# Row softmax on one core: row maximum added, tiles of sixteen rows per partition in three buffers

## The chip, the cores and the metric

The kernel runs on one core of one Trainium2 chip. The metric is the device time of one execution in microseconds (us); lower is better. VectorE is called DVE here, ScalarE is called ACT, and SP is the engine that issues the loads.

A run more than 1.5% above the fastest of the same kernel counts as slow.

## The reference

```python
x = randn(32, 512, 1024) as float32      # 16384 rows of 1024
temperature = 0.5

def reference(x, temperature):
    scaled = x / temperature
    shifted = scaled - max(scaled, axis=-1)
    e = exp(shifted)
    return e / sum(e, axis=-1)           # float32
```

67.1 MB are read and 67.1 MB are written.

## The kernel before

It leaves out the maximum. A tile has four rows per partition (2.1 MB, written 2 MB below, as the profile does), and eight tiles may be in flight. ACT does the exponential and the row sum, DVE the reciprocal and the multiplication.

```python
K_MAIN = 4; SPLIT_LAST = 4
data = tile_pool(name="data", bufs=8)
for it, (g0, K) in enumerate(sched):                 # 32 tiles
    xtile = data.tile([P, K, d], float32)
    nc.sync.dma_start(out=xtile, in_=xv)             # load, issued by SP
    for j in range(K):
        nc.scalar.activation(xtile[:, j, :], xtile[:, j, :], Exp,
                             scale=scale, accum_out=sums[:, j:j+1])
    nc.vector.reciprocal(recip, sums)
    for j in range(K):
        nc.vector.tensor_scalar_mul(xtile[:, j, :], in0=xtile[:, j, :],
                                    scalar1=recip[:, j:j+1])
    # ... cut: the last four tiles are stored in two halves
    nc.scalar.dma_start(out=ov, in_=xtile)           # store, issued by ACT
```

The program is plain text in this order, but the order in which an engine runs it need not be the order of the text: in the profile below ACT starts exponentials of tile 1 at 13.41 us and issues the store of tile 0 at 15.81 us.

The softmax here doesn't subtract the row's maximum and nothing guards it: scores larger than these inputs give would overflow.

Of the kernel before, what the change touches and what calls it, by code (L numbers as in the profile page):

```python
# [1 line left out]

# [4 lines left out]


@with_exitstack  # L10
def kernel(
    ctx: ExitStack,
    tc: tile.TileContext,
    x: bass.AP,
    temperature: bass.AP,
    out: bass.AP,
):
    nc = tc.nc
    scale = 1.0 / float(temperature)

    P = 128
    xf = x.flatten_outer_dims()
    of = out.flatten_outer_dims()
    n, d = xf.shape
    nrowgroups = n // P

    K_MAIN = 4
    SPLIT_LAST = 4
    sched = []
    g = 0  # L30
    while g < nrowgroups:
        k = min(K_MAIN, nrowgroups - g)
        sched.append((g, k))
        g += k
    ntiles = len(sched)

    data = ctx.enter_context(tc.tile_pool(name="data", bufs=8))
    stats = ctx.enter_context(tc.tile_pool(name="stats", bufs=16))

    for it, (g0, K) in enumerate(sched):  # L40
        rows = P * K
        r0 = g0 * P
        xv = xf[r0 : r0 + rows, :].rearrange("(p k) d -> p (k d)", p=P, k=K)
        ov = of[r0 : r0 + rows, :].rearrange("(p k) d -> p k d", p=P, k=K)

        xtile = data.tile([P, K, d], mybir.dt.float32)
        nc.sync.dma_start(out=xtile.rearrange("p k d -> p (k d)"), in_=xv)  # L47

        sums = stats.tile([P, K], mybir.dt.float32)
        recip = stats.tile([P, K], mybir.dt.float32)  # L50
        for j in range(K):
            nc.scalar.activation(  # L52
                xtile[:, j, :],
                xtile[:, j, :],
                mybir.ActivationFunctionType.Exp,
                scale=scale,
                accum_out=sums[:, j : j + 1],
            )
        nc.vector.reciprocal(recip, sums)  # L59
        for j in range(K):  # L60
            nc.vector.tensor_scalar_mul(  # L61
                xtile[:, j, :], in0=xtile[:, j, :], scalar1=recip[:, j : j + 1]
            )

        if it >= ntiles - SPLIT_LAST and K > 1:
            h = K // 2
            nc.scalar.dma_start(out=ov[:, :h, :], in_=xtile[:, :h, :])  # L67
            nc.sync.dma_start(out=ov[:, h:, :], in_=xtile[:, h:, :])
        else:
            nc.scalar.dma_start(out=ov, in_=xtile)  # L70


# [1 line left out]
_INS = ['x', 'temperature']  # L74
_OUTS = [((32, 512, 1024), 'float32')]
#: Inputs that are plain numbers.
_NUMBERS = {'temperature': 0.5}


# [26 lines left out]
```

## Time and profile before

| | before |
|---|---|
| time, median | 319.57 us (319.5 to 319.85) |
| span in the profile | 317.8 us |
| DVE busy / ACT busy | 93.4 us / 138.0 us |
| DMA engines busy, both queues | 52.9% + 46.3% = 99.2% of the span |

These lines are from the page of the kernel before: the busy time of each engine, the busy tenths of the DMA engines in 40 slices of the span, the rate in the same slices, the two DMA queues (q1 loads and some stores, q10 stores), and who owns the chain that ended last.

```profile
span 317.8 us, 636 instructions
DVE 93.4 (29%) x160; ACT 138.0 (43%) x257; POOL 0.2 (0%) x4
DMA  7999999999999999999999999999999999999996
GB/s 297 429 394 429 431 431 434 435 433 433 433 429 429 432 429 429 429 429 431 429 433 434 433 435 431 429 433 431 431 429 429 431 429 431 437 429 430 422 426 271
q1 hardware_dynamic: 5184, 71.31, 52.9%
q10 hardware_dynamic: 4608, 62.92, 46.3%
DMA 91%; ACT 1%; SPq 1%; DVE 1%; issue 0%; DVEq 0%; ACTq 0%
```

The DMA engines are busy from the first slice to the last. DVE and ACT are busy 29% and 43%.

The timeline of the kernel before, ACT and its DMA issues alone (start us, duration, engine, line, operation), shows the order of the text being left:

```profile
13.41 1.06 ACT L52 ACTIVATE xtile<-xtile 128x1024 f32<-128x1024 f32 x1 [0.62 <-DMA xtile<-in_x_dram]
...
15.50 1.04 ACT L52 ACTIVATE xtile<-xtile 128x1024 f32<-128x1024 f32 x1
15.81 0.37 ACTq L70 DMA_DIRECT2D out_dram<-xtile  x1
```

The exponential at 13.41 us belongs to tile 1. The DMA issue at 15.81 us is the store of tile 0, which the text lists before it.

### The profile page before, as it was taken

What the parts mean: (1) busy time and instruction counts of PE and PEld (TensorE: products, weight loads), DVE (VectorE), ACT (ScalarE), POOL (GpSimd) and SP (SyncE); (2) the same over time, 40 slices, a digit from 0 to 9 for tenths busy, and PEclk for the clock granted to TensorE, in tenths of its full rate; (3) what the DMA queues carried; (4) which work ended last, traced back from release to release, by engine and by line L of the source; (5) the groups of instructions that cost most, each with busy time, mean ns of one, the idle gap of its engine ahead of it and who ended that gap; (6) DMA issues with size and microseconds to landing.
All of it is one profiled execution on the core that took longest, in us unless ns stands there. A gap on an engine that the chain in (4) does not pass through costs nothing.

```text
span 317.8 us, 636 instructions
## 1 busy us (share of the span) xinstructions
DVE 93.4 (29%) x160; ACT 138.0 (43%) x257; POOL 0.2 (0%) x4
## 2 busy tenths in 40 slices
DVE  0352333312300517631333213333123003733300
ACT  1875334554321739655334553345543106852500
POOL 0000000000000000000000000000000000000000
DMA  7999999999999999999999999999999999999996
GB/s 297 429 394 429 431 431 434 435 433 433 433 429 429 432 429 429 429 429 431 429 433 434 433 435 431 429 433 431 431 429 429 431 429 431 437 429 430 422 426 271
DMA packets 9797, 134.26 MB, mean 422 GB/s; under 512 B 1088, under 2 KB 1088, under 8 KB 1088
## 3 DMA queue, kind: packets, MB, share of 16 engines
q1 hardware_dynamic: 5184, 71.31, 52.9%
q10 hardware_dynamic: 4608, 62.92, 46.3%
q14 instruction: 5, 0.04, 0.0%
HBM read 67.11 MB, written 67.11 MB: 422 GB/s over the span
## 4 chain that ended last, share of the span: by engine, by line
DMA 91%; ACT 1%; SPq 1%; DVE 1%; issue 0%; DVEq 0%; ACTq 0%
DMA xtile<-in_x_dram 55%; DMA out_dram<-xtile 36%; ACT xtile L52 1%; SPq L47 1%; DVE xtile L61 1%; DVEq L101 0%; ACTq L67 0%; DVE recip L59 0%; ACTq L52 0%; ACTq L70 0%
## 5 line engine op out<-in xcount | busy, mean ns | idle before, releaser
L52 ACT ACTIVATE xtile<-xtile 128x1024 f32<-128x1024 f32 x128 | 133.5, 1044 | 159.3 <-DMA xtile<-in_x_dram 158.2
L61 DVE TENSOR_SCALAR xtile<-xtile,recip 128x1024 f32<-128x1024 f32 x128 | 87.7, 749 | 1.1
L59 DVE RECIPROCAL recip<-sums 128x4 f32<-128x4 f32 x32 | 5.7, 178 | 206.5 <-ACT xtile L52 206.5
L52 ACT ACTIVATION_READ_ACCUMULATOR xtile<-xtile 128x1 f32 x128 | 23.8, 186 | 0.0
L52 ACT ACT_TABLE_LOAD x1 | 1.3, 1283 | 0.7 <-PEq L87 0.7
L87 POOL MEMSET const-bfloat16-1.0<- 128x1 bf16 x1 | 0.1, 101 | 0.0
L87 POOL MEMSET const-uint8-127<- 128x1 uint8 x1 | 0.1, 101 | 0.0
L87 POOL MEMSET const-float32-0.0<- 128x1 f32 x1 | 0.1, 98 | 0.2 <-issue 0.2
L87 POOL MEMSET const-float32-1.0<- 128x1 f32 x1 | 0.1, 98 | 0.0
## 6 DMA issues: line engine op xcount, KB each, us to landing
xtile<-in_x_dram SPq DMA_DIRECT2D x32, 2048.0 KB, 31.3
out_dram<-xtile ACTq DMA_DIRECT2D x28, 2048.0 KB, 24.2
out_dram<-xtile ACTq DMA_DIRECT2D x4, 1024.0 KB, 22.7
out_dram<-xtile SPq DMA_DIRECT2D x4, 1024.0 KB, 14.9
```

Of the source, the lines that this page charges most:

```text
L47: nc.sync.dma_start(out=xtile.rearrange("p k d -> p (k d)"), in_=xv)
L52: nc.scalar.activation(xtile[:, j, :], xtile[:, j, :], mybir.ActivationFunctionType.Exp, scale=scale, accum_out=sums[:, j : j + 1],)
L59: nc.vector.reciprocal(recip, sums)
L61: nc.vector.tensor_scalar_mul(xtile[:, j, :], in0=xtile[:, j, :], scalar1=recip[:, j : j + 1])
L87: nc = _bacc.Bacc("TRN2", target_bir_lowering=False, num_devices=1)
```

## The change

The intent is a numerically safe softmax (the maximum is subtracted), paid for with larger transfers: sixteen rows per partition, 8.4 MB per load and store, 64 KiB per partition in one piece, three buffers. Cut to its core:

```diff
+def _softmax_rows(nc, stats, xt, j0, n, scale):        # n = 4 rows
+    nc.vector.tensor_reduce(out=top, in_=xt[:, j0:j0+n, :], axis=X, op=max)
+    nc.vector.tensor_scalar_mul(bias, in0=top, scalar1=-scale)
+    for j in range(n):
+        nc.scalar.activation(..., Exp, bias=bias[:, j:j+1], scale=scale,
+                             accum_out=sums[:, j:j+1])
+    nc.vector.reciprocal(recip, sums)
+    for j in range(n):
+        nc.vector.tensor_scalar_mul(...)               # as before
 ...
-    K_MAIN = 4
+    plan = [[16]] * 7 + [[8, 8]]                       # rows per store, by tile
-    data = tile_pool(name="data", bufs=8)
+    data = tile_pool(name="data", bufs=3)
 ...
+        nc.sync.dma_start(out=xt, in_=xv)
+        for k in stores:
+            for a in range(j, j + k, 4):
+                _softmax_rows(nc, stats, xt, a, 4, scale)
+            nc.scalar.dma_start(out=ov[:, j:j+k, :], in_=xt[:, j:j+k, :])
```

A tile now has four groups of four rows. "The maxima of a tile" below are its four reductions on DVE, "the multiplies" its sixteen multiplications.

More of the change, by code (lines that the diff above doesn't have):

```diff
@@ L7 @@
 from concourse._compat import with_exitstack
+def _softmax_rows(nc, stats, xt, j0, n, scale):
+    f32 = mybir.dt.float32
+    P = xt.shape[0]
+    top = stats.tile([P, n], f32, name="top")
+    bias = stats.tile([P, n], f32, name="bias")
+    sums = stats.tile([P, n], f32, name="sums")
+    recip = stats.tile([P, n], f32, name="recip")
+    nc.vector.tensor_reduce(
+        out=top,
+        in_=xt[:, j0 : j0 + n, :],
+        axis=mybir.AxisListType.X,
+        op=mybir.AluOpType.max if scale > 0 else mybir.AluOpType.min,
+    )
+    nc.vector.tensor_scalar_mul(bias, in0=top, scalar1=-scale)
+    for j in range(n):
+        nc.scalar.activation(
+            xt[:, j0 + j, :],
+            xt[:, j0 + j, :],
+            mybir.ActivationFunctionType.Exp,
+            bias=bias[:, j : j + 1],
+            scale=scale,
+            accum_out=sums[:, j : j + 1],
+        )
+    nc.vector.reciprocal(recip, sums)
+    for j in range(n):
+        nc.vector.tensor_scalar_mul(
+            xt[:, j0 + j, :], in0=xt[:, j0 + j, :], scalar1=recip[:, j : j + 1]
+        )
 @with_exitstack
@@ L24 @@
     n, d = xf.shape
-    nrowgroups = n // P
-    K_MAIN = 4
-    SPLIT_LAST = 4
-    sched = []
-    g = 0
-    while g < nrowgroups:
-        k = min(K_MAIN, nrowgroups - g)
-        sched.append((g, k))
-        g += k
-    ntiles = len(sched)
-    data = ctx.enter_context(tc.tile_pool(name="data", bufs=8))
+    plan = [[16]] * 7 + [[8, 8]]
+    assert sum(sum(stores) for stores in plan) * P == n
+    data = ctx.enter_context(tc.tile_pool(name="data", bufs=3))
     stats = ctx.enter_context(tc.tile_pool(name="stats", bufs=16))
-    for it, (g0, K) in enumerate(sched):
+    r0 = 0
+    for stores in plan:
+        K = sum(stores)
         rows = P * K
-        r0 = g0 * P
-        xv = xf[r0 : r0 + rows, :].rearrange("(p k) d -> p (k d)", p=P, k=K)
+        xv = xf[r0 : r0 + rows, :].rearrange("(p k) d -> p k d", p=P, k=K)
         ov = of[r0 : r0 + rows, :].rearrange("(p k) d -> p k d", p=P, k=K)
-        xtile = data.tile([P, K, d], mybir.dt.float32)
-        nc.sync.dma_start(out=xtile.rearrange("p k d -> p (k d)"), in_=xv)
-        sums = stats.tile([P, K], mybir.dt.float32)
-        recip = stats.tile([P, K], mybir.dt.float32)
-        for j in range(K):
-            nc.scalar.activation(
-                xtile[:, j, :],
-                xtile[:, j, :],
-                mybir.ActivationFunctionType.Exp,
-                scale=scale,
-                accum_out=sums[:, j : j + 1],
-            )
-        nc.vector.reciprocal(recip, sums)
-        for j in range(K):
-            nc.vector.tensor_scalar_mul(
-                xtile[:, j, :], in0=xtile[:, j, :], scalar1=recip[:, j : j + 1]
-            )
-        if it >= ntiles - SPLIT_LAST and K > 1:
-            h = K // 2
-            nc.scalar.dma_start(out=ov[:, :h, :], in_=xtile[:, :h, :])
-            nc.sync.dma_start(out=ov[:, h:, :], in_=xtile[:, h:, :])
-        else:
-            nc.scalar.dma_start(out=ov, in_=xtile)
+        r0 += rows
+        xt = data.tile([P, K, d], mybir.dt.float32, name="xt")
+        nc.sync.dma_start(out=xt, in_=xv)
+        j = 0
+        for k in stores:
+            for a in range(j, j + k, 4):
+                _softmax_rows(nc, stats, xt, a, min(4, j + k - a), scale)
+            nc.scalar.dma_start(out=ov[:, j : j + k, :], in_=xt[:, j : j + k, :])
+            j += k
 _INS = ['x', 'temperature']
```

## The prediction

> **What bounds the kernel now.** The DMA engines. The slice row shows DMA at 9 tenths in all slices but the first and last; the window view gives 431 GB/s from 60 to 280 us. 67.1 MB are read and 67.1 MB written; at about 430 GB/s that is 312 us of a 317.8 us span. The chain of waits is 91% DMA; ACT is 43% busy, DVE 29%. [...]
>
> **What the change does.** Bytes stay the same. Each group of four rows adds a max reduction over 128x4096 and a tiny bias multiply on DVE. No trace shows one yet. [...] With the measured 0.18 us reciprocal and 2.74 us for four multiplies (timeline), DVE needs about 7.6 us per group, 30.5 us per 8.4 MB tile, 243 us in all. ACT needs 4.2 us per group; a tile costs DMA 2 x 19.5 = 39 us, so DMA remains busiest.
>
> In program order DVE would serialise with ACT (about 12 us per group, about 430 us with fill and drain). I don't expect this: before, in the timeline, tile 0's store is issued at 15.8 us behind three of tile 1's exponentials, although listed before them. So the program is reordered, and the next group's max should run under this group's exponentials.
>
> **Critical path.** Before, eight 2 MB buffers keep transfers queued all the time. After, three 8.4 MB buffers do not: a buffer must be loaded whole (19.5 us alone, up to 39 us when sharing with a store), computed (about 32 us), stored whole, and only then reloaded. I worked it out for two queues sharing 430 GB/s, with 2.7 us of DMA latency (first load before: 7.8 us to landing, 4.9 of them transfer):
> - First load lands near 23 us (8.5 before), first store issues near 55 us (15.8 before). Two further loads feed DMA until 65 us.
> - The first store is done near 81 us and load 3 can only then start: a DMA hole of a few us near 80 us.
> - Afterwards three buffers just fill DMA, unless DVE's order puts the next tile's first max before this tile's last multiplies: then stores wait for the next load, 8 us worse.
> - At the end the last tile takes 16 us to its first half store, then 15 us plus a 9.8 us store; DMA runs dry for 5 to 10 us.
>
> DMA idle in sum: about 10 us, up to 18 with the bad order. Estimated span 327 to 335 us; the time is 1.8 us above the span, as before.
>
> **Prediction: 330 us, 8 in 10 between 321 and 342. Faster by over 2%: 0.02; within 2%: 0.25; slower by over 2%: 0.73.**
>
> **What would show it right.** DVE busy 230 to 250 us (about 75%)[...]; ACT busy unchanged near 138 us; DMA 9 tenths in most slices, weak near 80 us and in the last 30 us; first exponential after 27 us; mean rate about 405 to 412 GB/s; SP's waits mostly loads waiting for stores.
>
> **What would make it wrong.** Program order kept on DVE (over 400 us). Next-tile max groups hoisted before the last multiplies (337 us or more). Loads favoured over stores in the DMA sharing, which would close the hole (about 322 us). A different rate for 64 KiB pieces.

No trace or run here shows the term for the time of one maximum. The sum for DVE came to 7.6 us per group and 243 us in all; 0.18 and 2.74 us of the 7.6 are measured (page and timeline of the kernel before), the rest is the term and the bias multiply. The 30.5 us per tile, the 32 us to compute a buffer, the 12 and 430 us of the program's order, the 55 and 81 us, the 230 to 250 us and the 16 and 15 us at the end carry that term too, and through them the prediction itself. In the changed kernel one maximum then took 4.41 us and its bias multiply 0.16 us. The 19.5, 39 and 9.8 us are estimates from bytes and 430 GB/s (431 measured), and the 2.7 us one from the kernel before: its first load, issued at 0.73 us, was in use 7.80 us later, and the next tile's 4.88 us after that (2.9 us by these figures).

## The result

The changed kernel takes 351.42 us (350.88 to 353.09, four fast runs) against 319.6 us. The ratio is 1.100, 95% interval 1.098 to 1.103. Ratios in this document are formed from the fast runs of both kernels in the same job, so they are not quite the ratio of the medians quoted. The time lies outside the range of 321 to 342 us.

From the page of the changed kernel, the lines that answer to those above, and the two groups that grew:

```profile
span 349.5 us, 566 instructions
DVE 231.6 (66%) x224; ACT 147.7 (42%) x257; POOL 0.2 (0%) x4
DMA  9989999896999969989899989998899995088998
GB/s 360 480 360 480 427 412 465 376 472 247 473 360 397 442 247 480 360 360 480 322 397 360 480 360 360 427 413 367 352 397 442 360 480 240 1 360 360 420 420 360
q1 hardware_dynamic: 1152, 67.11, 47.4%
q10 hardware_dynamic: 1296, 67.11, 44.4%
DMA 52%; DVE 36%; ACT 4%; issue 0%; DVEq 0%; ACTq 0%; SPq 0%
L25 ACT ACTIVATE xt<-xt,bias 128x1024 f32<-128x1024 f32 x128 | 145.1, 1134 | 153.4 <-DVE xt L35 101.8
L17 DVE TENSOR_REDUCE top<-xt 128x4 f32<-128x4096 f32 x32 | 140.3, 4412 | 87.5 <-DMA xt<-in_x_dram 87.5
```

Both queues together are busy 91.8% of 349.5 us, that is 320.8 us, where before it was 99.2% of 317.8 us, that is 315.3 us. So of the 31.7 us that the span grew, 26 us are DMA engines standing idle (28.7 us against 2.5) and between 5 and 6 us are the same bytes taking longer. (The single slices jump between 360 and 480: in a slice of 8.74 us these are 48 and 64 packets of 64 KiB, counted whole. Only means over longer stretches say something.) DVE is not the new limit: it is busy 66% and waits 87.5 us for loads. DVE nevertheless owns 36% of the chain that ended last, where it had 1%.

The windows of the changed kernel (stretch, its length, DVE busy, ACT busy, POOL busy, clock, DMA share, GB/s) show where the idle time is:

```profile
108.40:137.60 29.20, 29.03 (x28) 8.44 (x16) 0.00 (x0) 1.00 0.93 395
137.60:168.00 30.40, 12.14 (x5) 18.04 (x31) 0.00 (x0) 1.00 0.92 379
...
193.60:222.70 29.10, 28.88 (x28) 10.00 (x18) 0.00 (x0) 1.00 0.94 396
222.70:253.20 30.50, 12.50 (x4) 18.32 (x32) 0.00 (x0) 1.00 0.91 378
...
279.00:293.90 14.90, 14.83 (x6) 9.42 (x18) 0.00 (x0) 1.00 0.97 422
293.90:308.80 14.90, 14.14 (x23) 0.00 (x0) 0.00 (x0) 1.00 0.00 1
```

One hole of 15 us at 294 us, with no byte moving while DVE works, and 6 to 9% missing in stretches all along. The timeline of DVE (and the DMA issues) in the changed kernel shows the reason, here between the load of tile 3 and the store of tile 2 ("..." and the gaps between the maxima stand for short bias and reciprocal instructions and for other multiplies, left out):

```profile
98.14 0.34 ACTq L78 DMA_DIRECT2D out_dram<-xt  x1
108.43 8.74 DVE L17 TENSOR_REDUCE top<-xt 128x4 f32<-128x4096 f32 x2 [10.32 <-DMA xt<-in_x_dram]
117.16 4.41 DVE L17 TENSOR_REDUCE top<-xt 128x4 f32<-128x4096 f32 x1
121.55 4.41 DVE L17 TENSOR_REDUCE top<-xt 128x4 f32<-128x4096 f32 x1
...
126.28 2.74 DVE L35 TENSOR_SCALAR xt<-xt,recip 128x1024 f32<-128x1024 f32 x4
...
134.87 2.74 DVE L35 TENSOR_SCALAR xt<-xt,recip 128x1024 f32<-128x1024 f32 x4
137.64 0.34 ACTq L78 DMA_DIRECT2D out_dram<-xt  x1
```

DVE idles 10.32 us until tile 3 has landed, at 108.43 us. Then it runs all four maxima of tile 3 (17.5 us), and only then the multiplies of tile 2 (11.7 us). Tile 2's store goes out at 137.64 us, 29.2 us after a load that it has no use for. At the end it is the same: the last load lands at 279.07 us, the store of tile 6 is issued at 308.45 us, and from 293.9 us on nothing is left to move until then. The first half of tile 7 is stored only at 317.62 us, 38.6 us after its load. All four maxima stand ahead in this way from tile 1's multiplies on; before tile 0's last multiplies stand only two of tile 1's.

The waits of the changed kernel, in total (engine, line, what it waited for, us, times, longest), say the same in three lines; the last is from the view of SP's own queue. In the first, ACT's next exponential stands behind a store in ACT's queue, and that store waits for the multiplies (ACT stops for 17.24 us until the store of 137.64 us has gone out):

```profile
ACT xt L25 <- DVE xt L35: 101.8, 6, 17.4
DVE top L17 <- DMA xt<-in_x_dram: 87.5, 6, 22.7
SPq L72 <- DMA out_dram<-xt: 249.5, 5, 79.6
```

Loads wait for stores (a buffer must be free), stores wait for the next tile's load (through DVE's order). The three buffers are tied together.

### The profile page after: what moved, and what is told of

Its sections match the earlier page's. It is cut to its first block, busy times and chain, and to the rows that moved or that the text cites. A ratio compares the mean times of both kernels' runs of the same rounds, so it can differ in the third digit from the quotient of the medians.

```text
span 349.5 us, 566 instructions
## 1 busy us (share of the span) xinstructions
DVE 231.6 (66%) x224; ACT 147.7 (42%) x257; POOL 0.2 (0%) x4
## 4 chain that ended last, share of the span: by engine, by line
DMA 52%; DVE 36%; ACT 4%; issue 0%; DVEq 0%; ACTq 0%; SPq 0%
DMA xt<-in_x_dram 29%; DMA out_dram<-xt 24%; DVE top L17 22%; DVE xt L35 13%; ACT xt L25 4%; DVE recip L33 0%; DVE bias L23 0%; DVEq L110 0%; ACTq L78 0%; SPq L72 0%
## 5 line engine op out<-in xcount | busy, mean ns | idle before, releaser
L25 ACT ACTIVATE xt<-xt,bias 128x1024 f32<-128x1024 f32 x128 | 145.1, 1134 | 153.4 <-DVE xt L35 101.8
L17 DVE TENSOR_REDUCE top<-xt 128x4 f32<-128x4096 f32 x32 | 140.3, 4412 | 87.5 <-DMA xt<-in_x_dram 87.5
L35 DVE TENSOR_SCALAR xt<-xt,recip 128x1024 f32<-128x1024 f32 x128 | 87.7, 749 | 1.2 <-issue 0.3
L25 ACT ACTIVATION_READ_ACCUMULATOR xt<-xt,bias 128x1 f32 x128 | 23.9, 187 | 0.0
L23 DVE TENSOR_SCALAR bias<-top 128x4 f32<-128x4 f32 x32 | 4.4, 156 | 0.0
```

The costliest lines, as they stand in the source:

```text
L17: nc.vector.tensor_reduce(out=top, in_=xt[:, j0 : j0 + n, :], axis=mybir.AxisListType.X, op=mybir.AluOpType.max if scale > 0 else mybir.Al ...
L23: nc.vector.tensor_scalar_mul(bias, in0=top, scalar1=-scale)
L25: nc.scalar.activation(xt[:, j0 + j, :], xt[:, j0 + j, :], mybir.ActivationFunctionType.Exp, bias=bias[:, j : j + 1], scale=scale, accum_o ...
L35: nc.vector.tensor_scalar_mul(xt[:, j0 + j, :], in0=xt[:, j0 + j, :], scalar1=recip[:, j : j + 1])
```

## The experiments

Theories:

- **Order**: the time goes because maxima of later tiles stand on DVE before the multiplies that a store needs.
- **Buffer**: three whole-tile buffers, each loaded, computed and stored as one, cost the time whatever the order.
- **Piece**: 64 KiB pieces move slower than 16 KiB ones.
- **Maximum**: the reduction itself costs the time.

All kernels gave correct results, except the three copies. The diffs are cut to their core.

### Order alone (e1_order, e1_again)

```diff
     for a in range(j, j + k, 4):
-        _softmax_rows(nc, stats, xt, a, ...)
+        with tc.issue_after(prev.ins):   # queue behind tile t-1's last multiply, same engine
+            last = _softmax_rows(nc, stats, xt, a, ...)
+    prev = last
```

> The changed kernel, with one thing added: on DVE every instruction of tile t+1 is queued behind the last multiply of tile t. Order theory (the store of tile t waits for the load of tile t+1 because the maxima of t+1 stand before the multiplies of t): 333 to 342 us against 351, and the stores are issued about 30 us after their own tile's load lands instead of 29 us after the next tile's. Buffer theory (three whole-tile buffers cost the time whatever the order): 348 to 353 us. Piece theory (64 KiB pieces move slower): 348 us or more.

> The kernel of e1_order once more, since its profiled run was the slow one (348.5 us against 331.8). Expected: 330 to 333 us, and in the profile stores issued about 30 us after the landing of their own tile, with the last load landing near 285 us instead of 301.5.

Measured: 331.84 us median of four runs. The fast ones are 330.76 to 331.92 us, ratio 1.037 (1.035 to 1.039). The profiled run took 348.5 us. Repeated: one timed run of 330.64 us, and the profiled one again slow, 342.02 us. So the order is worth 20 us of the 32, which the order theory asked for (1 us more than its range said) and the buffer and piece theories denied. There is no profile of this kernel's fast time. Why its profiled runs are slow is not settled. The same order in smaller pieces (d1_order_16k, below) has a fast profile, and it shows what was expected here: tile 3 has landed at 123.08 us, and its store is issued 30.1 us later, before any work on tile 4.

```profile
123.08 8.74 DVE L17 TENSOR_REDUCE top<-xt 128x4 f32<-128x4096 f32 x2 [10.34 <-DMA xt<-in_x_dram]
...
153.18 0.38 ACTq L83 DMA_DIRECT2D out_dram<-xt  x1
```

The edge is set on DVE, but ACT's order changed with it: in the changed kernel three exponentials of tile 3 (from 117.28 us) stand on ACT before the store of tile 2, in d1_order_16k none of the next tile does. In the changed kernel these three are done at 120.7 us and the store waits for DVE until 137.6 us, so DVE decides there. ACT's order by itself was not set in any run; e3_nomax below has it without the maximum, and there it is worth 8 us at the most.

### The same program with small tiles (e2_rows4), and with the order set (e5_rows4_ahead1)

```diff
-plan = [[16]] * 7 + [[8, 8]]; bufs=3
+plan = [[4]] * 31 + [[2, 2]]; bufs=8
```

> The changed program with four rows per partition, eight buffers and the last tile stored in two halves, as small as the kernel before; the row maximum stays, so DVE stays near 232 us busy. Order and buffer theories: the maximum alone is hidden under the DMA and the time is 319 to 324 us. If the maximum itself costs the time: 340 us or more.

Measured: 374.9 us, ratio 1.173. The number of the order and buffer theories was missed by 51 us, and that of the maximum theory (340 us or more) is met; the next run decides. The order of the compiled program on DVE shows what I had not looked at. Names ending in 385 are tile 18, those ending in 277 tile 12:

```
61 L33 Reciprocal recip_282<-sums_281 128x4
62 L17 TensorReduce top_387<-xt_385 128x4
63 L35 TensorScalarPtr xt_277<-xt_277,recip_282 128x1024 x4
```

The maximum of tile 18 stands before the multiplies of tile 12. With eight buffers in flight the store of a tile waits for a load up to six tiles later. Its page and waits:

```profile
DMA  8999999999869978958995899598599769919998
...
DVE top L17 <- DMA xt<-in_x_dram: 113.6, 21, 9.8
```

Then one thing was added: the maximum of tile t+2 is queued behind the multiplies of tile t, so that one maximum at most stands ahead.

```diff
+with tc.issue_after(muls[-2].ins):
     last = _softmax_rows(...)
```

> The kernel of e2_rows4 (four rows, eight buffers, with maximum, 374.9 us) with one thing added: on DVE the maximum of tile t+2 is queued behind the multiplies of tile t, so that only one maximum stands ahead. Order theory: the whole 55 us go, 319 to 323 us, with DVE still near 232 us busy. If the maximum itself, or DVE and DMA getting in each other's way, cost e2_rows4 its time: 345 us or more.

Measured: 319.15 us (319.1 to 319.18), ratio 0.998 (0.997 to 1.000). All 55.7 us are gone, by order alone, so the order theory was right for e2_rows4 too. From its page and its DVE timeline:

```profile
span 317.4 us, 703 instructions
DVE 236.8 (75%) x227; ACT 150.2 (47%) x257; POOL 0.2 (0%) x4
DMA  8999999999999999999999999999999999999996
...
147.96 4.42 DVE L17 TENSOR_REDUCE top<-xt 128x4 f32<-128x4096 f32 x1 [2.26 <-DMA xt<-in_x_dram]
...
152.69 2.74 DVE L35 TENSOR_SCALAR xt<-xt,recip 128x1024 f32<-128x1024 f32 x4
157.66 4.42 DVE L17 TENSOR_REDUCE top<-xt 128x4 f32<-128x4096 f32 x1 [2.22 <-DMA xt<-in_x_dram]
```

DVE carries the full maximum, 236.8 us of work, and the DMA slices look like those of the kernel before. The maximum theory falls: the reduction fits under the traffic entirely. The wait for the next tile's load (2 MB) is small, 2.26 and 2.22 us in these lines, and the DMA engines stay at 9 tenths meanwhile.

### No maximum (e3_nomax)

```diff
-    nc.vector.tensor_reduce(out=top, ...)
-    nc.vector.tensor_scalar_mul(bias, ...)
-            bias=bias[:, j:j+1],
```

> The changed kernel without maximum and bias; sixteen rows, 64 KiB pieces and three buffers stay. Order theory: nothing of a later tile can stand before a store on DVE, so 319 to 329 us. Buffer theory: still 340 us or more. Piece theory: DMA bytes per busy time about 2% below the kernel before, 325 us or more with DMA at 9 tenths nearly everywhere.

Measured: 327.85 us, ratio 1.027 (1.024 to 1.031). With nothing to stand in front of the multiplies on DVE, sixteen rows and three buffers cost 8 us, not 32. The other 24 us came with the maximum. In e1_order the maximum stays and only the order changes, and it takes 331.84 us: about 20 of these 24 us came with the place in the order. On ACT, exponentials of the next tile still stand in front of a store here: tile 2's multiplies are done at 98.9 us, but its store leaves at 122.65 us, 0.2 us after tile 3 has landed. So a store that merely waits for the next load costs at most these 8 us; in the changed kernel 29 us of DVE work come between that load and the store. The number of the piece theory (325 us or more, with DMA at 9 tenths nearly everywhere) is met here as well: the DMA engines are busy 98.3% of 325.7 us, 320 us against 315 us before. So some 5 of the 8 us are the same bytes taking longer.

### Transfers in four parts, with the order and without (e9_pieces, e10_pieces_only)

```diff
-nc.sync.dma_start(out=xt, in_=xv)
+for a in range(0, K, 4):
+    nc.sync.dma_start(out=xt[:, a:a+4, :], in_=xv[:, a:a+4, :])
-plan = [[16]] * 7 + [[8, 8]]
+plan = [[4] * 4] * 8            # stores in fours too; the buffers stay
```

> The kernel of e1_order with each tile loaded and stored in four transfers of 2 MB, buffers as before (three of sixteen rows). If what is left over the kernel before (12 us) is the waiting for whole 8.4 MB transfers at the start, between tiles and at the end, it goes to 318 to 325 us. If it is the three large buffers themselves, 328 us or more.

> The fourth corner of a square: the changed kernel with loads and stores in four transfers of 2 MB, but the order on DVE left as it came out. Corners so far: neither 351.4, order alone 331.8, both 320.7 us. Order theory: maxima of the next tile still stand before stores of this one, so pieces alone do not cure it: 330 to 352 us. If coarse transfers were the cause and the order only a part of it: 325 us or less.

Measured: 320.73 us with the order (ratio 1.003) and 343.65 us without (ratio 1.075). The four corners, medians in us:

| | order as it came out | order set |
|---|---|---|
| whole transfers of 8.4 MB (64 KiB pieces) | 351.4 | 331.8 |
| four transfers of 2 MB (16 KiB pieces) | 343.7 | 320.7 |

The order is worth 19.6 and 22.9 us, the smaller transfers 7.8 and 11.1 us. Together they give back 30.7 of the 31.8 us. The three large buffers, with the maximum, cost the remaining 1.1 us.

The second row differs from the first in more than the size of a transfer: its pieces are 16 KiB, and a store can leave after four rows. The pieces are not what it gains by: the kernels below with whole transfers in 16 KiB pieces take 350.4 us (e4_16k) and 333.8 us (d1_order_16k), so against them the split is worth 6.7 and 13.1 us. Where the 13.1 us were lost, the fast profiles show: the DMA engines idle for 16.0 us of d1_order_16k (busy 95.2% of 332.8 us) and for 3.8 us of e9_pieces (98.8% of 319.0 us), and in d1_order_16k they are busy 3% of the last 11.9 us before the last tile's first store (299.0 to 310.9 us). In the left column the compiled order on DVE is not the same in both rows (in e10_pieces_only multiplies stand between the maxima, as at 68.00 and 76.44 us of its DVE timeline), so its 7.8 us are not of the transfers alone.

### Piece size with nothing else changed (e4_16k)

```diff
-xv = xf[...].rearrange("(p k) d -> p k d", p=P, k=16)     # 64 KiB runs
+xv = xf[...].rearrange("(c p k) d -> p c k d", p=P, k=4)  # 16 KiB runs, still one transfer
```

> The changed kernel with the rows laid out so that each transfer still carries 8.4 MB but in 16 KiB contiguous pieces. Order theory: 347 to 353 us, as the waits are the same. Piece theory: the rate rises from 418 to 426 GB per busy second and the time falls by 6 us or more, to 345 us or less.

Measured: 350.39 us against 351.42, so the order theory's number. Here the waits decide, and the piece size is worth 1.0 us: the rate per busy time is 415 GB/s in both (table below).

### One maximum ahead (e7_ahead1), and the two orders in 16 KiB pieces (d1_order_16k, d2_ahead1_16k)

e7_ahead1 makes the order that the prediction called the bad one: the edge of e5_rows4_ahead1 put into the changed kernel, so that one group's maximum at most stands ahead. The other two are e1_order and e7_ahead1 in the layout of e4_16k. With one ahead, the groups of a tile also alternate on DVE (maximum, multiplies, maximum, ...), where the other orders do all four maxima of a tile first.

> The changed kernel (sixteen rows, three buffers) in the order that the prediction called the bad one: the maximum of the next tile's first four rows alone stands before the last multiplies of a tile. The sum that gave the prediction says 8 us more than with nothing ahead (e1_order, 331.8 us): 335 to 342 us, and below the 351.4 us of four maxima ahead. If only the count of maxima ahead within DVE matters and not the wait for the load, it is within 2 us of e1_order.

> The kernel of e1_order (331.8 us) in the layout of e4_16k: transfers of 8.4 MB, but in 16 KiB pieces. If side by side 64 KiB pieces slow each other, as c1_copy64 (329.1) against c2_copy16 (320.7) says, the rate in the middle rises towards 428 GB per busy second and the time falls by 5 to 9 us, to 323 to 327 us. If e1_order's remaining 12 us are waits only: 330 to 333 us. The profiled run should no longer be a slow one.

> The kernel of e7_ahead1 (356.3 us) in the layout of e4_16k. The sum behind the prediction, which holds the rate at 430 GB/s, gives about 337 us for this order. If the 64 KiB pieces account for what it missed: 334 to 342 us. If the loss is one of waits or of simultaneous starts, whatever the pieces: 350 us or more.

| order on DVE | 64 KiB pieces | 16 KiB pieces |
|---|---|---|
| all four maxima ahead (as changed) | 351.4 | 350.4 |
| one maximum ahead | 356.3 | 325.0 |
| none ahead | 331.8 | 333.8 |

e7_ahead1 missed its number by 14 us at the least, d1_order_16k came out 7 us above what the piece theory asked for (and 0.8 us above "waits only"), and d2_ahead1_16k 9 us below its lowest number. In 64 KiB pieces one maximum ahead is the worst order, in 16 KiB pieces it is the best. What the profile of e7_ahead1 shows is a load and a store issued at the same moment (SP's and ACT's DMA issues in its timeline), against a pair 7 us apart:

```profile
125.03 0.33 SPq L74 DMA_DIRECT2D xt<-in_x_dram  x1
125.05 0.36 ACTq L82 DMA_DIRECT2D out_dram<-xt  x1
...
177.01 0.33 SPq L74 DMA_DIRECT2D xt<-in_x_dram  x1
184.12 0.34 ACTq L82 DMA_DIRECT2D out_dram<-xt  x1
```

The load of 125.03 us has landed by 176.81 us, when DVE starts on it: 52 us. The load of 177.01 us took 35 us. In d2_ahead1_16k a load and a store also start within 1 us (125.43 and 124.54 us), and that load needs 40.5 us. The packet records of the traces give the mean duration of a packet and the rate per busy time (bytes over summed durations, times 16 engines), each from 60 to 280 us on the clock of those records:

```
kernel            piece    load packet   store packet   GB per busy s
before            16 KiB    0.61 us       0.61 us       429
e5_rows4_ahead1   16 KiB    0.61 us       0.61 us       429
changed           64 KiB    2.62 us       2.42 us       415
e4_16k            16 KiB    0.65 us       0.61 us       415
e7_ahead1         64 KiB    2.79 us       2.50 us       398
d2_ahead1_16k     16 KiB    0.62 us       0.62 us       422
c1_copy64         64 KiB    2.59 us       2.47 us       414
c2_copy16         16 KiB    0.62 us       0.61 us       428
```

The usual packet of 64 KiB takes 2.42 us, four times 0.61 us, with a store beside it or not. The means are higher because of slow packets (more than 10% above the usual) that come in bunches. A load has 128 packets. In the changed kernel each load from tile 3 on has 30 to 32 slow ones: about 16, as many as there are DMA engines, at its start, and about 16 when a store is issued beside it; its seven whole stores have one in all. In e7_ahead1 the load of 125.03 us has 80, all through it, and the store issued with it has 50. In d2_ahead1_16k the load of 125.43 us has none. So the pieces of 64 KiB that were slow throughout belong to a load and a store that start together; that the two directions run side by side is not enough. And 16 KiB pieces have bunches of slow packets too (79 to 86 of 512 in each load of e4_16k from tile 3 on).

### Copies (c1_copy64, c2_copy16, c3_copy_small)

All arithmetic is left out and x is copied to the output: through two buffers of 8.4 MB in 64 KiB or 16 KiB pieces, or through eight of 2 MB.

> Wrong on purpose: no arithmetic, x is copied to the output through two buffers of 8.4 MB in 64 KiB pieces, so that a load and a store always start within 3 us of each other and each waits for the other's buffer. At 430 GB/s the sum is about 339 us (a first load of 23, seven rounds of 39 + 2.7, a last store of 22). If a load and a store that run side by side slow each other's packets, as in the profiles of e7_ahead1 and e1_order (381 GB per busy second): 365 us or more.

> Wrong on purpose: c1_copy64 with the rows laid out in 16 KiB pieces and transfers of 8.4 MB as before. If the slowing in c1_copy64 is one of 64 KiB pieces: 339 us. If it comes from two whole-tile transfers starting together: the same as c1_copy64 within 5 us.

> Wrong on purpose: no arithmetic, x is copied to the output through eight buffers of 2 MB, as the kernel before moves its data. This is the floor of the traffic: 316 to 319 us, with packets of 0.61 us throughout, at most 3 us below the kernel before.

Measured: 329.08, 320.75 and 318.58 us. The small copy is the fastest that this traffic ran here; the kernel before is 1.1 us above it and e5_rows4_ahead1 0.6 us, so a version that moves the same bytes would have to beat this copy by 5 us to win 2%. Whole-tile copies in 64 KiB pieces cost 8.3 us more than in 16 KiB pieces, so in this copy the large pieces are slower. My two sums for c1_copy64 were both wrong, and so were those for c2_copy16: I had counted 2.7 us in each of seven rounds (the forecast's estimate from the first load of the kernel before, 7.8 us to landing with 4.9 of them transfer). Without it the sum is 320 us, which c2_copy16 fits; that a second transfer under way hides this time is my reading, not shown.

## Why the prediction was wrong

**Right.** DMA bounds the kernel before (99.2% busy, 318.58 us as a copy). The maximum takes 4.41 us per group (4412 ns for 128x4096 elements in the page). DVE is busy 231.6 us (230 to 250 said), and DVE is not the limit (66% busy). The program's order was not kept. The first store was issued at 60.2 us (55 said) and load 3 at 81.7 us (81 said). That load 3 fits is partly luck: the store left 5 us late, behind two of tile 1's maxima, and took about as much less than I had given it. SP's waits are loads waiting for stores (249.5 us).

**Wrong, and decisive: "the next group's max should run under this group's exponentials", with the loss bounded by "unless DVE's order puts the next tile's first max before this tile's last multiplies: then stores wait for the next load, 8 us worse".** I had read from the profile that the order of the text is not kept, and then assumed the helpful amount of it, one group. In the changed kernel, from tile 1 on, all four maxima of the next tile stand before all multiplies of this one. A store is issued 29 us after the next tile's load, not at the end of its own work. The prediction did name such an order among what would make it wrong, at "337 us or more", but it had counted one maximum ahead of the last multiplies and 8 us for it, not four maxima ahead of all sixteen. Setting the order alone gives back 19.6 us (e1_order), 22.9 us with smaller transfers, and 55.7 us with small tiles (e5_rows4_ahead1).

**Wrong in size: "8 us worse" for one maximum ahead.** It measured 24.5 us in 64 KiB pieces (e7_ahead1 against e1_order), and the opposite sign, 8.8 us better, in 16 KiB pieces. The sum held the rate at 430 GB/s at all times; it was 398 GB/s per busy time in e7_ahead1. (The two orders differ in more than one maximum: the groups of a tile alternate in one and not in the other.)

**Wrong in size: the end.** "At the end the last tile takes 16 us to its first half store" and "DMA runs dry for 5 to 10 us": it took 38.6 us, with a hole of 15 us, because tile 6's multiplies were also still to come. With the order set it still took 23.5 us (287.41 to 310.90 us in d1_order_16k), so the 16 us were too few in any case.

**Wrong, small.** ACT was not unchanged: 147.7 us, since an exponential with a per-partition bias took 1134 ns instead of 1044 ns without one in the kernel before (1.04 us in e3_nomax, which has no bias either). ACT owns 4% of the chain that ended last.

**Half right.** I had said that larger pieces would gain next to nothing. The most they gained was 2 us (331.8 against 333.8 us, order set), and they could lose: 8 us as a copy, 31 us with one maximum ahead (e7_ahead1 against d2_ahead1_16k), 1 us in the changed kernel itself (e4_16k). Whole-tile transfers cost 7 to 13 us. With the order set it is for a reason that I had in the sum (queues that run dry: 16.0 us of idle DMA against 3.8), about the 10 us that I predicted.

**Open.** Why the 64 KiB packets of a load and a store that start together are slow is not shown by any run; it is not always so (e1_again has a pair 0.3 us apart, the store first at 208.58 us, whose load has no slow packet). Neither is why one maximum ahead beats none by 8.8 us in 16 KiB pieces, nor why the profiled runs of e1_order are 11 to 17 us slower than its timed ones. (In both, the fourth load is slow throughout and lands at 133 us, where d1_order_16k has it at 123 us; whether the timed runs avoid this is not on record.) My guess is that with whole-tile transfers the time depends on how loads and stores happen to fall against each other; I did not find a rule for it.

## What to carry to other kernels

When work is added to an engine with room to spare, ask where it stands in that engine's queue, not only how long it takes. Here four maxima that waited for the next load, in front of the multiplies that the next store waited for, cost 19.6 us in large tiles and those of up to six later tiles cost 55.7 us in small ones; a single one ahead cost 24.5 us in 64 KiB pieces and gained 8.8 us in 16 KiB ones. Read the compiled order before costing a change, and set the order where it matters; here that alone moved one and the same program from 374.9 to 319.15 us, with the maximum fully hidden. Where DMA bounds a kernel, try several moderate transfers queued instead of few whole-tile ones: here that took 13 us off the kernel with the order set and 16 KiB pieces (333.8 to 320.7 us), 12 of them idle DMA time.
